# Two of the eight sums over partitions of a modulation vector: accumulating transfers in DRAM instead of TensorE transposes

## The chip, the cores and the metric

The kernel runs on one core of one Trainium2 chip. The metric is the device time of one execution in microseconds (us). Three runs of the kernel before took 1219.54, 1219.89 and 1221.70 us; their median is 1219.89 us. The profile is that of one more execution. Times inside it are us from the start of its span.

## What is computed

The reference is one layer of a diffusion backbone over 512 latent tokens of 1024 channels, with 256 context tokens beside them. Cut to what matters here:

```
mod = silu(c) @ w_mod + b_mod              # 1024 -> 6 * 1024
sh1, sc1, gt1, sh2, sc2, gt2 = split(mod, 6)
x = x + gt1 * token_mixer(modulate(x, norm1_g, sh1, sc1), ...)
x = x + gt2 * conv_ffn(modulate(x, norm2_g, sh2, sc2))
out = rmsnorm(x, final_g)
```

`gt2` is the last 1024 of the 6144 numbers. It is a gate: each of its numbers scales one channel of the ConvFFN's result. So it is needed only at the very end, while its share of the product with `w_mod` can be formed at any time before.

## The kernel before

All matrix products run on TensorE (PE) in float32r, with each operand split into a high part (a cast on ScalarE, ACT) and a low part (a subtraction on VectorE, DVE), so that each product is three matmuls. Weights stream from DRAM on SyncE's queue (SP) in pieces of 512 KB into three buffers `wraw`; `load` (lines 186 to 210) issues a piece, and `split` (line 181) makes `whi` and `wlo` of it. `run` goes through a list of steps and loads each step's weights one or two pieces ahead. The steps' order is written out by hand with `weave`, which deals the items of a second list evenly among those of a first. A scheduler then places the instructions on each engine's queue by its own estimate, except where a step is marked as ordered by hand.

The last two stages matter here. In the **up stage** (`up_step`, t = 0 to 21; matmuls on lines 237, 238 and 240) each step multiplies the normed tokens with two pieces of `w_up`, 48 matmuls with a free size of 512, and DVE and ACT apply a convolution of three taps, an activation and the product of the two halves (lines 1391 to 1395 and 1976 to 1986). In the **down stage** (`down_step`; matmuls on lines 2215 to 2217) seven products follow, in six pieces of weights each, as `w_down` is multiplied by a scheme with fewer products. Sums of its weights were formed earlier, in the attention stage, by accumulating transfers on GpSimd's queue (line 164). The first down weights go through `whi` and `wlo` too, later ones also through `dnraw` and `dnw`.

The second modulation (the last 4096 of the 6144 numbers) is computed on DVE, not on PE: `m_step(i)`, i = 0 to 31, loads a piece of `w_mod`, multiplies its rows by `silu(c)`, one number per partition, and adds up in an accumulator `acc` (a buffer of the tag `tm`, 128 x 512). Four steps make one column group `cg` of 512 columns (lines 794 and 796). What is left is the sum over the 128 partitions. For that PE transposes the four 128 x 128 blocks into a bank of PSUM (line 800), DVE reduces it to four columns of `mod2` (line 802) and adds the bias (line 803). Groups 6 and 7 (i = 24 to 31) hold `gt2`; their steps are dealt among the up steps 0 to 17.

`row_tiles` (from line 2056) makes rows of the gate: it copies and negates the eight columns into `g2c`, transposes them on PE (line 2060), copies the result out of PSUM (line 2061), stores 4 KB to DRAM (`g2_d`, line 2062, printed as `g_d`) and loads them back, spread over all partitions (line 2068, into the tags `q2` and `ssq`, printed as `rowq` and `rowssq`). It also loads two rows of `final_g` (line 2067), the second into a buffer of the tag `tm`. The gate rows are first used in the middle of the down stage, by GpSimd on line 2091.

Of the kernel before, what the change touches and what calls it, by code (L numbers as in the profile page):

```python
# [9 lines left out]
F32 = mybir.dt.float32  # L10
# [3 lines left out]
ALU = mybir.AluOpType  # L14
# [4 lines left out]
P = 128  # L19
# [8 lines left out]
V_BMOD = 0  # L28
# [11 lines left out]
def raw(ap):  # L40
    return ap.bitcast(F32)
# [3 lines left out]
def tile_hybrid_layer(  # L45
# [32 lines left out]
    V, S, G, T = nc.vector, nc.scalar, nc.gpsimd, nc.tensor  # L78
# [5 lines left out]
    dpool = ctx.enter_context(tc.tile_pool(name="dpool", bufs=1, space=DRAM))  # L84
# [25 lines left out]
    def misb():  # L110
        return bank("mis")
# [3 lines left out]
    def tmp(tag):  # L115
        return tpool.tile([P, 512], F32, tag=tag, name=tag, bufs=TMP[tag])
# [27 lines left out]
    for j, t in enumerate((wdn[0], DSUMS[1], DSUMS[2], DSUMS[5], DSUMS[4], wdn[1], wdn[3])):  # L144
        for u in range(DU):
            n = min(2, DK - 2 * u) * HC
# [11 lines left out]
    QUEUED = mybir.DependencyInfo(mybir.DependencyClass.NoSync, mybir.DependencyReason.SCHED_ONLY)  # L158
# [22 lines left out]

    def split(r, n, hi, lo):
        F["cast"] = S.copy(hi[:, :n], r[:, :n])  # L183
        return V.tensor_tensor(lo[:, :n], r[:, :n], raw(hi[:, :n]), ALU.subtract)  # L184

    ELSEWHERE = {}
    SCALED = {("dn", 40), ("dn", 41)}
# [1 line left out]
    def load(key):  # L189
        r, n = load_raw(key)  # L190
        if key[0] == "m":
            return r
        if key in SCALED:
            for z in range(0, n, 512):
                V.tensor_tensor(r[:, z : z + 512], r[:, z : z + 512], rows_["g"][1], ALU.mult)
        if key in ELSEWHERE:
            hi, lo = ELSEWHERE[key]()
            split(r, n, hi, lo)
            return hi, lo
        if key[0] == "dn" and key[1] % 4 > 1:  # L200
            if "dnw" not in F:
                F["dnw"] = hpool.tile([P, 2, 2, 1024], F32R, tag="hll", name="dnw")
            hi, lo = (F["dnw"][:, key[1] % 2, i, :] for i in range(2))
        else:
            hi = wpool.tile([P, 1024], F32R, tag="whi", name="whi", bufs=2)
            lo = wpool.tile([P, 1024], F32R, tag="wlo", name="wlo", bufs=2)
        split(r, n, hi, lo)
        return hi, lo
# [13 lines left out]
    def weave(a, b):  # L222
        r, n, m = [], len(a), len(b)
        for i in range(n):
            r.append(a[i])
            r += b[i * m // n : (i + 1) * m // n]
        return r
# [18 lines left out]
    vec = cpool.tile([P, NV], F32, name="vec")  # L246
# [13 lines left out]
    mod2 = cpool.tile([P, 32], F32, name="mod2")  # L260
# [165 lines left out]
    with tc.tile_pool(name="spool", bufs=1) as sp:  # L426
# [235 lines left out]
        r = {}  # L662
        cq = tmp("te")[:, :LC]
        for j in range(KT):
# [46 lines left out]
            x = ("hi", "lo") if j >= NU else ("hh", "hl")  # L711
# [31 lines left out]
        for n in range(2):  # L743
            for j in range(KT):
                x = ("hi", "lo") if j >= NU else ("hh", "hl")
# [33 lines left out]
        return [("g", i)], fn  # L779

    macc = {}

    def m_step(i):
        cg, kk = i // 4, i % 4

        def fn(r):
            if kk == 0:
                macc[0] = tmp("tm")
            acc = macc[0]
            for u in range(2):  # L790
                k = 2 * kk + u
                sc = csil[:, k, 0:1]
                if k == 0:
                    V.tensor_scalar_mul(acc, r[:, 0:512], sc)
                else:
                    V.scalar_tensor_tensor(acc, r[:, u * 512 : u * 512 + 512], sc, acc, ALU.mult, ALU.add)  # L796
            if kk == 3:
                ps = misb()
                for c in range(4):
                    T.transpose(ps[:, c * P : (c + 1) * P], acc[:, c * P : (c + 1) * P], ident)  # L800
                z = slice(4 * cg, 4 * cg + 4)
                V.tensor_reduce(mod2[:, z], ps.rearrange("p (c q) -> p c q", c=4), axis=AX.X, op=ALU.add)
                V.tensor_tensor(mod2[:, z], mod2[:, z], vec[:, V_BMOD + 16 + 4 * cg : V_BMOD + 20 + 4 * cg], ALU.add)

        return [("m", i)], fn
# [71 lines left out]
    Q, F = {}, {}  # L877
# [1152 lines left out]
    def x1_turn(c):  # L2030

        def fn():
            t = tmp("te")
            V.transpose(t, x1[c // 4][:, c % 4, :])
            for a in range(4):
                o = x1_d[:, c * P + 32 * a : c * P + 32 * a + 32].rearrange("(f i) j -> i f j", i=32)
                nc.sync.dma_start(o, t[32 * a : 32 * a + 32, :].rearrange("i (f j) -> i f j", j=32))

        return [], fn
# [10 lines left out]
    x1_rows = [], x1_load  # L2050
# [3 lines left out]
    rows_ = {}  # L2054

    def row_tiles():
        V.tensor_copy(g2c[:, 0:4], mod2[:, 24:28])
        V.tensor_scalar_mul(g2c[:, 4:8], mod2[:, 28:32], -1.0)
        ps, t = misb(), tmp("te")
        T.transpose(ps[0:8, 0:P], g2c, ident)  # L2060
        V.tensor_copy(t[0:8, 0:P], ps[0:8, 0:P])
        nc.sync.dma_start(g2_d.rearrange("(c p) -> c p", p=P), t[0:8, 0:P])
        tiles = [hpool.tile([P, HC], F32, tag=t, name="row" + t) for t in ("q2", "ssq", "rbc4")] + [tmp("tm")]
        rows_["g"], rows_["f"] = tiles[:2], tiles[2:]
        for i in range(2):
            z = slice(HC * i, HC * i + HC)
            nc.sync.dma_start(rows_["f"][i], fg_d[z].partition_broadcast(P))
            nc.sync.dma_start(rows_["g"][i], g2_d[z].partition_broadcast(P))
# [150 lines left out]
    def down_step(j, u):  # L2219
        tail = j == 6 and u == 2  # L2220

        def fn(*w):
# [40 lines left out]
        + [([("out", o) for o in (5, 6, 7)], out_last), ([], close_c1)]  # L2263
        + weave(
            weave([up_step(t) for t in range(18)], msteps[24:]) + [up_step(t) for t in range(18, NFF)],
            [([], lambda: None)] * 6 + [x1_turn(c) for c in range(8)] + [x1_rows] + [([], lambda: None)] * 4 + [([], row_tiles)] + [([], lambda: None)] * 2,
        )
        + [down_step(j, u) for j in range(7) for u in range(3 if j == 6 else DU)],
        early=("g", 15),
# [86 lines left out]
```

## Time and profile before

| | us |
|---|---|
| median of three runs | 1219.89 |
| the profiled execution | 1219.4 |
| its span, first to last instruction | 1217.6 |
| PE busy | 1208.7 |
| DVE busy | 924.4 |
| ACT busy | 679.6 |
| GpSimd (POOL) busy | 204.8 |

A row of the profile in order of time gives the start, the duration, the engine, the line of the kernel, the operation with its tiles (out <- in), how many such instructions are merged, and in brackets how long the engine was idle before and what released it. PE is the matmul itself and PEld the weight load that runs ahead of it. A matmul's row is longer than the distance to the next row, as matmuls are pipelined. `x2` behind a row means two instructions; its duration is then that of both. SPq is the queue from which SyncE issues transfers. Buffer numbers are left out of names (`x_d` is `x1_d`, `mod` is `mod2`).

### The profile page before, as it was taken

The page shows a single profiled execution, that of the slowest core. Times are in us where ns is not written, and L with a number is a line of the kernel's source. Part 1 is how long each engine was busy: PE and PEld are TensorE (multiplying, and loading weights), DVE is VectorE, ACT ScalarE, POOL GpSimd, SP SyncE. Part 2 cuts the span into 40 slices and gives each one's busy share as a digit, 9 for nine tenths or more (in the row PEclk, how much of TensorE's full clock was granted, in tenths as well). Part 3 has the DMA queues.
Part 4 walks back from the last instruction along what each step waited for, and adds up shares of the span by engine and source line. Part 5 has one row for each costly group of instructions (what it writes and reads, how often), then busy time and mean ns, then how long its engine had stood idle before and what let it go on. Part 6 is the DMA issues. An engine that isn't in the chain of part 4 may idle for free.

```text
span 1217.6 us, 17462 instructions
## 1 busy us (share of the span) xinstructions
PE 1208.7 (99%) x6296; PEld 993.7 (82%) x6296; DVE 924.4 (76%) x1499; ACT 679.6 (56%) x1263; POOL 204.8 (17%) x223
## 2 busy tenths in 40 slices
PE   9999999999999999999999999999999999999997
PEld 6798888888878868778777778888988888888886
DVE  5857888888566688797896867677787777768777
ACT  5557787778544367486575664223534334346653
POOL 0000121100003544252451631000200000000021
PEclk9999999999999999999999999999999999999999
DMA  9645889844758535346376558777265534337652
GB/s 371 259 137 184 160 242 261 170 148 129 175 160 247 169 87 181 108 133 194 104 167 202 172 188 277 233 238 242 55 159 135 190 109 135 119 115 234 193 187 88
DMA packets 122920, 214.71 MB, mean 176 GB/s; under 512 B 26312, under 2 KB 68368, under 8 KB 122832
## 3 DMA queue, kind: packets, MB, share of 16 engines
q1 hardware_dynamic: 110256, 187.09, 49.0%
q0 software_dynamic: 12288, 26.22, 9.5%
q8 instruction: 50, 0.82, 0.3%
q14 instruction: 38, 0.31, 0.1%
q10 hardware_dynamic: 288, 0.27, 0.1%
HBM read 187.26 MB, written 43.85 MB: 190 GB/s over the span
## 4 chain that ended last, share of the span: by engine, by line
PE 96%; DVE 1%; issue 1%; ACT 1%; DMA 1%; POOL 0%; SPq 0%; POOLq 0%; DVEq 0%; ACTq 0%
PE acc L237 20%; PE acc L240 20%; PE acc L238 20%; PE score L958 3%; PE po L1007 3%; PE pt L994 2%; PE mis L580 2%; PE mis L1687 2%; PE mis L1559 2%; PE mis L1695 1%; PE mis L2217 1%; PE mis L2216 1%; PE mis L2215 1%; PE acc L2217 1%; PE acc L2216 1%; PE acc L2215 1%
## 5 line engine op out<-in xcount | busy, mean ns | idle before, releaser
L183 ACT CAST whi<-wraw 128x1024 fp32r<-128x1024 f32 (+1 forms) x115 | 120.3, 1047 | 160.0 <-PE acc L238 107.0
L184 DVE TENSOR_TENSOR wlo<-wraw,whi 128x1024 fp32r<-128x1024 f32 (+1 forms) x115 | 143.6, 1249 | 68.1 <-ACT whi L183 65.6
L237 PE MATMUL acc<-hlh,whi 128*128 128x512 f32 x472 | 194.0, 411 | 0.0
L238 PE MATMUL acc<-hll,whi 128*128 128x512 f32 x472 | 185.0, 392 | 0.0
L240 PE MATMUL acc<-hlh,wlo 128*128 128x512 f32 x472 | 184.9, 392 | 0.0
L237 PE MATMUL acc<-mh,whi 128*128 128x512 f32 x368 | 143.6, 390 | 0.0
L238 PE MATMUL acc<-ml,whi 128*128 128x512 f32 x368 | 143.2, 389 | 0.0
L240 PE MATMUL acc<-mh,wlo 128*128 128x512 f32 x368 | 143.2, 389 | 0.0
L240 PEld LDWEIGHTS acc<-hlh,wlo 128*128 128x128 f32 x472 | 88.6, 188 | 19.6
L237 PEld LDWEIGHTS acc<-hlh,whi 128*128 128x128 f32 x472 | 88.8, 188 | 18.0 <-issue 2.8
L238 PEld LDWEIGHTS acc<-hll,whi 128*128 128x128 f32 x472 | 88.9, 188 | 17.3 <-issue 2.4
L240 PEld LDWEIGHTS acc<-mh,wlo 128*128 128x128 f32 x368 | 69.1, 188 | 14.5
L237 PEld LDWEIGHTS acc<-mh,whi 128*128 128x128 f32 x368 | 69.1, 188 | 14.4
L238 PEld LDWEIGHTS acc<-ml,whi 128*128 128x128 f32 x368 | 69.1, 188 | 14.2
L967 DVE CUSTOM_DVE_ANT_0 p<-score,winm,nsink 128x512 f32<-128x512 f32 (+1 forms) x64 | 51.8, 810 | 15.4 <-PE score L958 13.9
L1392 DVE SCALAR_TENSOR_TENSOR ta<-acc,half,ta 128x511 f32<-128x511 f32 (+1 forms) x66 | 43.8, 664 | 22.6 <-ACT ta L1391 22.4
L1391 ACT ACTIVATE ta<-acc,half 128x512 f32<-128x512 f32 (+1 forms) x66 | 46.7, 708 | 25.2 <-PE acc L240 23.9
L974 ACT ACTIVATE p<-p,mneg 128x512 f32<-128x512 f32 (+1 forms) x64 | 49.7, 777 | 15.4 <-DVE mneg L967 14.8
L164 POOL DMA_DIRECT2D dsum<-wdn x24 | 25.4, 1143 | 193.0 <-DVE wlo L1091 171.7
L1002 DVE TENSOR_TENSOR ptl<-pt,pth 128x512 fp32r<-128x512 f32 x72 | 47.5, 685 | 8.5 <-ACT pth L998 7.7
L796 DVE SCALAR_TENSOR_TENSOR tm<-wraw,csil,tm 128x512 f32<-128x512 f32 x56 | 43.6, 778 | 13.0 <-DMA wraw<-wm 12.3
L237 PE MATMUL acc<-hch,whi 128*128 128x256 f32 x176 | 53.2, 302 | 0.0
(444 smaller groups left out, 2994.0 us busy)
## 6 DMA issues: line engine op xcount, KB each, us to landing
wraw<-wup SPq DMA_DIRECT2D x44, 512.0 KB, 3.6
dsum<-wdn POOLq DMA_DIRECT2D x24, 704.0 KB, 8.9
wraw<-wm SPq DMA_DIRECT2D x32, 512.0 KB, 4.0
fb<-cs_d SPq DMA_DIRECT2D x32, 512.0 KB, 6.6
wraw<-wx SPq DMA_DIRECT2D x24, 512.0 KB, 3.7
wm<-wm SPq DMA_DIRECT2D x16, 512.0 KB, 8.2
wraw<-wz SPq DMA_DIRECT2D x16, 512.0 KB, 4.2
wraw<-wos SPq DMA_DIRECT2D x16, 512.0 KB, 4.7
```

The costliest lines, as they stand in the source:

```text
L183: F["cast"] = S.copy(hi[:, :n], r[:, :n])
L184: return V.tensor_tensor(lo[:, :n], r[:, :n], raw(hi[:, :n]), ALU.subtract)
L237: T.matmul(ps, wh, xh[:, k0 + k, :], start=a, stop=False)
L238: T.matmul(ps, wh, xl[:, k0 + k, :], start=False, stop=False)
L240: T.matmul(ps, wl, xh[:, k0 + k, :], start=False, stop=b)
L796: V.scalar_tensor_tensor(acc, r[:, u * 512 : u * 512 + 512], sc, acc, ALU.mult, ALU.add)
L958: T.matmul(ps[:, o : o + len(z) * P], Q[h][:, b * P : (b + 1) * P], k[:, j, z[0] * P : (z[-1] + 1) * P], start=v == 0 and o % 512 in (0, P ...
L967: V.tensor_tensor_reduce(p[:, :w], d["ps"][i][:, o0 : o0 + w], m, op0=ALU.add, op1=ALU.min, scale=1.0, scalar=nsink[:, h : h + 1], accum_o ...
L974: S.activation(p, p, AF.Exp, bias=d["mneg"][:, i : i + 1], scale=-1.0, accum_out=d["den"][:, i : i + 1])
L1002: V.tensor_tensor(d["ptl"][x], d["pt"][x], raw(d["pth"][x]), ALU.subtract)
L1391: S.activation(o[:, :n], ps[:, :n], AF.Identity, scale=hcol(base_w, stride + i), bias=hcol(base_b, i))
L1392: x = V.scalar_tensor_tensor(o[:, 1:n], ps[:, 0 : n - 1], hcol(base_w, i), o[:, 1:n], ALU.mult, ALU.add)
```

## The change

For the column groups 6 and 7 the sum over partitions is no longer formed on PE and DVE. The accumulator is stored to a tile in DRAM, 128 rows of 512. Then seven transfers on GpSimd's queue each add the upper half of the rows that are left to the lower half, in place: 64 rows, 32, 16, 8, 4, 2 and 1. A ninth transfer loads the one row that remains into four columns of `mod2`. The bias is added by a new function `folded`, on DVE and behind a split: for group 6 in the last m step, for group 7 at the head of `row_tiles`. `row_tiles` itself stands two places later in the list that is dealt among the up steps (21 empty or other items ahead of it instead of 19, of 22).

```diff
 
     def split(r, n, hi, lo):
         F["cast"] = S.copy(hi[:, :n], r[:, :n])
-        return V.tensor_tensor(lo[:, :n], r[:, :n], raw(hi[:, :n]), ALU.subtract)
+        F["sub"] = V.tensor_tensor(lo[:, :n], r[:, :n], raw(hi[:, :n]), ALU.subtract)
+        return F["sub"]
...
     macc = {}
+    FOLDS = {cg: dpool.tile([P, 512], F32, name="fold%d" % cg) for cg in (6, 7)}
+
+    def fold(cg, acc):
+
+        d, n = FOLDS[cg], P // 2
+        G.dma_start(d, acc)
+        while n:
+            G.dma_start(d[0:n, :], d[n : 2 * n, :], accum_op=ALU.add, max_dma_last_dim=512)
+            n //= 2
+        G.dma_start(mod2[:, 4 * cg : 4 * cg + 4], d[0, :].rearrange("(c p) -> p c", p=P))
+
+    def folded(cg):
+        z = slice(4 * cg, 4 * cg + 4)
+        x = V.tensor_tensor(mod2[:, z], mod2[:, z], vec[:, V_BMOD + 16 + 4 * cg : V_BMOD + 20 + 4 * cg], ALU.add)
+        tc.add_manual_dep(x.ins, F["sub"].ins.name, QUEUED, reason="behind a split")
...
-            if kk == 3:
+            if i == 31:
+                folded(6)
+            if kk == 3 and cg in FOLDS:
+                fold(cg, acc)
+            elif kk == 3:
                 ps = misb()
...
     def row_tiles():
+        folded(7)
         V.tensor_copy(g2c[:, 0:4], mod2[:, 24:28])
...
-            [([], lambda: None)] * 6 + [x1_turn(c) for c in range(8)] + [x1_rows] + [([], lambda: None)] * 4 + [([], row_tiles)] + [([], lambda: None)] * 2,
+            [([], lambda: None)] * 6 + [x1_turn(c) for c in range(8)] + [x1_rows] + [([], lambda: None)] * 6 + [([], row_tiles)],
```

**GpSimd, the second chain.** Here are the nine transfers of group 7 on its queue and the instruction behind them (`fold_765` is the tile in DRAM, `mod_94` is `mod2`; shapes are those of the transfers as they are cut). Each of them waits for the one ahead.

```order
L788 DMA fold_765<-tm 128x512
L790 DMA fold_765<-fold_765 256x128
L790 DMA fold_765<-fold_765 128x128
L790 DMA fold_765<-fold_765 64x128
L790 DMA fold_765<-fold_765 32x128
L790 DMA fold_765<-fold_765 16x128
L790 DMA fold_765<-fold_765 16x64
L790 DMA fold_765<-fold_765 16x32
L792 DMA mod_94<-fold_765 128x4x1
L2112 TENSOR_TENSOR te<-te,rowq_10795 128x512
```

Before, the queue had none of these rows: behind the eight subtractions `ml<-ta,mh` of the normalization came the last row, line 2091 there. Nine more rows, for group 6, now stand ahead of the ones shown. On PE the row `mis<-ident,tm 128x128 x4` is gone at the two places where groups 6 and 7 ended; nothing has taken its place.

**DVE and PE at the end of the up stage.** On DVE the last up step before, from the low part of the first down weight:

```order
L184 TENSOR_TENSOR wlo<-wraw,whi 128x1024
L1954 TENSOR_TENSOR fs_8819<-fx_8815,fs_8819 128x256
L1392 SCALAR_TENSOR_TENSOR ta<-acc,half,ta 128x511
L1395 SCALAR_TENSOR_TENSOR ta<-acc,half,ta 128x511
L1977 SCALAR_TENSOR_TENSOR ta<-tb,ta 128x512
```

and the same place now, to the low part of the second down weight:

```order
L184 TENSOR_TENSOR wlo<-wraw,whi 128x1024
L1974 TENSOR_TENSOR fs_8821<-fx_8817,fs_8821 128x256
L1412 SCALAR_TENSOR_TENSOR ta<-acc,half,ta 128x511
L796 TENSOR_TENSOR mod_94<-mod_94,vec 128x4
L1415 SCALAR_TENSOR_TENSOR ta<-acc,half,ta 128x511
L2079 TENSOR_SCALAR g2c<-mod_94 128x4
L1997 SCALAR_TENSOR_TENSOR ta<-tb,ta 128x512
L2082 COPY te<-mis 8x128
L184 TENSOR_TENSOR wlo<-wraw,whi 128x1024
```

The bias add of group 7 (line 796 of the changed kernel), which waits for the ninth transfer, the scaling of `g2c` and the copy of the transposed `g2c` have moved here from the steps of t = 17 and t = 19. On PE the transpose of `g2c` now stands between the last matmul of the up stage and the first of the down stage, where before the two stood side by side:

```order
L241 MATMUL acc<-mh,wlo 128x512
L2081 MATMUL mis<-ident,g2c 8x128
L2236 MATMUL mis<-whi,fs_8820 128x512
L2237 MATMUL mis<-whi,fs_8820 128x512
L2238 MATMUL mis<-wlo,fs_8820 128x512
```

**SP's queue** from the last piece of `w_mod` on, before:

```order
L177 DMA wraw<-wm 128x1024
L177 DMA wraw<-wup 128x1024 x4
L2067 DMA tm<-fg_d 128x512
L177 DMA wraw<-wup 128x1024 x4
L2062 DMA g_d<-te 8x128
L177 DMA wraw<-wdn 128x1024
L2068 DMA rowq_10631<-g_d 128x512
L2068 DMA rowssq<-g_d 128x512
L177 DMA wraw<-wdn 128x1024 x3
L177 DMA dnraw<-wdn 128x512
```

and now:

```order
L177 DMA wraw<-wm 128x1024
L177 DMA wraw<-wup 128x1024 x2
L2088 DMA tm<-fg_d 128x512
L177 DMA wraw<-wup 128x1024 x6
L177 DMA wraw<-wdn 128x1024 x4
L177 DMA dnraw<-wdn 128x512
L2083 DMA g_d<-te 8x128
L177 DMA dnraw<-dsum_75 128x1024
L177 DMA wraw<-wdn 128x1024
L2089 DMA rowq_10795<-g_d 128x512
L2089 DMA rowssq<-g_d 128x512
L177 DMA wraw<-dsum_75 128x1024 x2
```

The row of `final_g` into `tm` has moved ahead of two weight loads, and now waits for the store of `tm` on GpSimd's queue. The store of `g2_d` and the two gate rows stand behind the first four down weights, the gate rows behind the fifth as well.

## The prediction

> **What bounds the kernel now.** I read the page first (busy shares), then the busy time in stretches of the program, then the list of waits, and at last the instructions in order of time around the two places that the change touches.
>
> ```profile
> span 1217.6 us, 17462 instructions
> PE 1208.7 (99%) x6296; PEld 993.7 (82%) x6296; DVE 924.4 (76%) x1499; ACT 679.6 (56%) x1263; POOL 204.8 (17%) x223
> 950.00:1000.00 50.00, 50.00 (x224) 41.36 (x224) 37.86 (x56) 19.94 (x27) 0.00 (x0) 1.00 0.39 128
> 1050.00:1080.00 30.00, 30.00 (x135) 24.81 (x135) 22.11 (x34) 13.06 (x18) 0.00 (x0) 1.00 0.33 107
> 1110.00:1150.00 40.00, 40.00 (x179) 33.10 (x178) 29.96 (x33) 25.77 (x33) 0.00 (x0) 1.00 0.74 238
> ```
>
> The last three rows are stretches: length, then the busy time of PE, PEld, DVE, ACT and POOL, the granted clock (1.00), the DMA share and GB/s. Up stage (950 to 1105) and down stage (1105 to 1209) look alike: PE is busy in all of 50, 30 and 40 us. So a matmul-side instruction taken out there shortens the run by what it costs PE; DVE, ACT, POOL and the transfers matter only where they come so late that PE waits. DVE has 20 to 25% to spare.
>
> **The change, part by part.**
>
> *Eight transposes less on PE.* Two of the eight groups at L800 go, the ones for column groups 6 and 7. Their neighbourhood in order of time:
>
> ```profile
> 954.81 0.39 PE L240 MATMUL acc<-mh,wlo 128*128 128x512 f32 x1
> ...
> 962.29 0.39 PE L240 MATMUL acc<-mh,wlo 128*128 128x512 f32 x1
> 962.53 0.60 PE L800 MATMUL mis<-ident,tm 128*128 128x128 f32 x4
> 962.88 0.48 PE L237 MATMUL acc<-mh,whi 128*128 128x512 f32 x1
> ...
> 966.19 0.39 PE L240 MATMUL acc<-mh,wlo 128*128 128x512 f32 x1
> ```
>
> ```profile
> 1060.71 0.39 PE L240 MATMUL acc<-mh,wlo 128*128 128x512 f32 x1
> 1060.94 0.60 PE L800 MATMUL mis<-ident,tm 128*128 128x128 f32 x4
> ...
> 1064.61 0.39 PE L240 MATMUL acc<-mh,wlo 128*128 128x512 f32 x1
> ```
>
> From the L240 at 954.81 to that at 962.29 are 11 triples, 33 matmuls: 7.48 / 33 = 0.2267 us each. From 962.29 to 966.19 there are 15 matmuls, 15 x 0.2267 = 3.40, but 3.90 us pass: the group costs **0.50 us**, not the 0.60 that its row shows, because matmuls overlap, and some of it lies in a slower pace just behind. From 1060.71 to 1064.61 it is again 15 matmuls in 3.90 us: 0.50. Sum: **-1.0 us**, all on the path. The small transpose of g2c only changes its place; it costs what it cost.
>
> *DVE.* Two reductions of PSUM go, and the two adds of the bias stay. That is work off the path; I count nothing.
>
> *The chain on GpSimd's queue.* Per column group nine transfers, each waiting for the one ahead: the store of acc, seven sums, and the load of four columns into mod2. GpSimd has nothing else to do then:
>
> ```profile
> POOL te L2091 <- DVE te L2113: 290.2, 1, 290.2
> ```
>
> Its next instruction waits 290.2 us for the down stage, so nothing is held up behind the nine. The question is only whether the load into mod2 lands before DVE reaches the bias add, since a late one stops DVE, and with it PE. The second chain (column group 7) has the shorter time. It starts when the last accumulation ends:
>
> ```profile
> 1044.92 1.54 DVE L796 SCALAR_TENSOR_TENSOR tm<-wraw,csil,tm 128x512 f32<-128x512 f32 x2 [0.16 <-DMA wraw<-wm]
> 1063.97 0.15 DVE L803 TENSOR_TENSOR mod<-mod,vec 128x4 f32<-128x4 f32 x1
> 1064.76 0.16 DVE L2058 TENSOR_SCALAR g2c<-mod 128x4 f32<-128x4 f32 x1
> 1102.18 0.74 DVE L1392 SCALAR_TENSOR_TENSOR ta<-acc,half,ta 128x511 f32<-128x511 f32 x1
> 1102.96 0.75 DVE L1395 SCALAR_TENSOR_TENSOR ta<-acc,half,ta 128x511 f32<-128x511 f32 x1
> 1105.08 0.39 PE L2215 MATMUL mis<-whi,fs 128*128 128x512 f32 x1
> ```
>
> Start 1044.92 + 1.54 = 1046.46. In the new order the bias add stands between L1392 and L1395 of the last up step, so at 1102.18 + 0.74 = 1102.92: 56.5 us, less 0.5 since the group at 1060.94 is gone. Behind it come L1395 (0.75) and the scaling of g2c (0.16); 1102.92 + 0.15 + 0.75 + 0.16 = 1103.98, while PE wants its transpose at 1105.08, so 1.1 us more is free: the chain may take about **57 us** at no cost. What it takes, the trace shows only by relatives:
>
> ```profile
> dsum<-wdn POOLq DMA_DIRECT2D x24, 704.0 KB, 8.9
> fb<-cs_d SPq DMA_DIRECT2D x32, 512.0 KB, 6.6
> L1444 POOL DMA_DIRECT2D xs_d<-xb x32: 582/620/692, 376.3 to 412.5; - x32
> DMA to landing us min/median/max: 1.8/3.5/7.8
> 392.84 4.93 POOL L1444 DMA_DIRECT2D xs_d<-xb  x8 [4.81 <-DVE xb L1435]
> 399.08 0.77 POOL L1453 DMA_DIRECT2D xs<-xs_d  x1 [1.31 <-DMA xs_d<-xb]
> ```
>
> Rows 1 to 4 give the time from issue to landing. Small stores on this queue (rows 3 and 4) take 1.8 to 7.8, in the middle 3.5. Rows 5 and 6 show one step of a dependent pair: the last store is issued at 392.84 + 4.93 - 0.62 = 397.15, a reader at 399.08, a step of 1.9 if it waited for the last one. Sums of 704 KB are among the transfers of row 1 (8.9); here they are 128 KB and less. I take 3.5 for the store and for each sum, being nearest in size, and 6.6 (row 2, also many short pieces) for the load of columns: 3.5 + 24.5 + 6.6 = 34.6 us, over at 1081, with 22 us to spare. Ends: 9 x 1.8 = 16 us, no cost; and 7.8 + 7 x 8.9 + 7.8 = 77.9 us, 21 us of stall. Chain 6 starts 98 us earlier, before 949, and its add stands near 1059, so even 77.9 us fit.
>
> A row first: the 620 ns of an issue (row 3 above) were measured while DVE worked beside it. The Trainium skill, SBUF — State Buffer, speaks against the change in the sections "A bandwidth-pool intuition that's wrong (but worth ruling out)" and "Who interferes with whom": a transfer issued by GpSimd whose descriptors are kept back by a DVE copy took about 3100 ns where it takes 620 alone. By that the nine would take an estimated 22 us more, 57 in all, just at the limit: no loss yet, but nothing to spare. The same section names copy, cast and tensor_scalar as the operations that do so and leaves tensor_tensor out, and the trace sides with this: 582 to 692 ns, no row near 3100.
>
> *SP's queue.* The row load of final_g now stands two weight loads earlier and waits for the store out of tm instead of for PE; the store of g2 and the two gate rows move from the up stage into the start of the down stage.
>
> ```profile
> 1046.49 11.65 SPq L177 DMA_DIRECT2D wraw<-wup  x4
> 1061.57 0.33 SPq L2067 DMA_DIRECT2D tm<-fg_d  x1
> 1083.81 0.34 SPq L2062 DMA_DIRECT2D g_d<-te  x1
> 1086.03 0.33 SPq L2068 DMA_DIRECT2D rowq<-g_d  x1
> rowq<-g_d SPq DMA_DIRECT2D x1, 256.0 KB, 4.0
> rowssq<-g_d SPq DMA_DIRECT2D x1, 256.0 KB, 4.2
> ```
>
> The store out of tm should land by 1046.46 + 3.5 = 1050 (1054.3 at 7.8). Two of the four loads in the first row now come behind it, and the last of the four leaves at 1057.8 today; even 1054.3 lets it leave then, and today SP stands until 1061.57 without a gap on PE: I count nothing. SP waited 1086.03 - 1083.81 = 2.2 us from the store of g2 to its first reader. Now that store leaves at about 1105.8, once DVE has copied the transposed g2c, so the rows leave at about 1108, 0.5 MB right behind the load of the fifth down weight:
>
> ```profile
> 1107.39 0.33 SPq L177 DMA_DIRECT2D wraw<-wdn  x1
> 1111.37 1.05 ACT L183 CAST whi<-wraw 128x1024 fp32r<-128x1024 f32 x1 [1.17 <-DMA wraw<-wdn]
> 1113.34 1.22 DVE L184 TENSOR_TENSOR wlo<-wraw,whi 128x1024 fp32r<-128x1024 f32 x1
> 1115.96 0.39 PE L2215 MATMUL mis<-whi,fs 128*128 128x512 f32 x1
> ```
>
> That weight is the tightest: ACT waits for its landing, DVE is done at 1114.56, and PE needs the low part in its third matmul, at 1115.96 + 2 x 0.2267 = 1116.41. If the rows push the landing back by 512 KB at the 238 GB/s of the stretch, 2.2 us, the cast ends at 1114.6 and the low part at 1115.9: still in time, I take 0. Were it the whole 4.2 us of a row's landing, the low part would be ready at 1111.37 + 4.2 + 1.05 + 1.22 = 1117.84, 1.4 us late; a gain is excluded, as nothing leaves the bus there.
>
> **Sum.** The profiled execution took 1219.4 (span 1217.6 and 1.8 around it). 1219.4 - 1.0 = 1218.4; the median of the runs, 1219.89, lies 0.5 above that execution, so **1218.9**.
>
> **The rivals.**
> - *The chain is late.* Place: the bias add of group 7 on DVE, with g2c's transpose on PE at the head of the down stage behind it. With 3.5 and 6.6 for the first and last transfer it decides from (57 - 10.1) / 7 = 6.7 us per sum. At 8.9 the chain takes 72.4, 15.4 too long: 1218.9 + 15.4 = **1234.3**. For it: a sum must read two operands, and the only sums in the trace are among the slow row. Against it: those move 704 KB, and a small store is seen to land in 1.8.
> - *Gate rows in the crowd.* 1.4 us of stall at the fifth down weight: **1220.3**. For it: a DMA share of 0.74, and ACT already waits there for a landing. Against it: 1.85 us of slack, and the rows leave behind that weight, not ahead of it.
> - *The gain doesn't arrive.* If transfers, not free buffers, set the pace at the start of the down stage, PE arrives 1.0 us early and waits: **1219.9**. Against it: PE is busy in all of 40 us, and SP's loads there are released by DVE.
>
> **How the numbers follow.** The forecast gets 0.70, the late chain 0.13, the crowded rows 0.10, the lost gain 0.07. About 0.2%, 2.4 us, is what a measurement of this kernel can tell from no change (1217.5 to 1222.3). Within it lie the rows, the lost gain, 0.01 of the late chain (late by under 3 us) and 0.66 of the forecast, whose other 0.04 is the chance that scatter or a dearer transpose carries it past the bound: same 0.84, faster 0.04, slower 0.12. The range 1217.8 to 1221.0 takes in the forecast with the scatter of the runs and both small rivals; the late chain up to 21 us stays outside, within the 2 in 10.
>
> **What would show it.** PE rows: six groups of four transposes instead of eight, and PE still without idle time from 950 to 1209. GpSimd's queue: a step of about 3.5 us, the load into mod2 done near 1081; a wait of DVE's bias add on a DMA of more than a few tenths, and PE idle ahead of g2c's transpose, would prove the late chain. The gate rows: leaving near 1107, and the fifth cast landing by 1113.5; a PE gap near 1115 would prove the crowd. I'd be wrong altogether if the sums cost a time that doesn't shrink with their size.

## The result, and the profile after

The changed kernel takes **1218.28 us** (median of 21 runs, 1217.51 to 1219.53); the kernel before took 1219.81 in 21 runs beside it (1219.06 to 1221.70). The ratio is 0.9987, with a 95% interval of 0.9981 to 0.9993: 1.5 us less, between 0.9 and 2.3. The forecast was 1218.9, within 0.2% of before. The profiled execution took 1217.93 (before 1219.4).

The page's head of the changed kernel, then two of its stretches (columns as in the prediction):

```profile
span 1216.2 us, 17466 instructions
PE 1207.5 (99%) x6288; PEld 992.7 (82%) x6288; DVE 922.6 (76%) x1497; ACT 679.5 (56%) x1263; POOL 219.1 (18%) x241
```

```profile
1050.00:1080.00 30.00, 30.00 (x134) 24.85 (x133) 22.17 (x34) 12.46 (x18) 6.47 (x8) 1.00 0.44 121
1110.00:1150.00 40.00, 40.00 (x179) 33.10 (x178) 29.66 (x33) 26.55 (x33) 0.00 (x0) 1.00 0.76 253
```

PE has eight instructions fewer and is still busy in all of 30 and 40 us; GpSimd has eighteen more and works 6.47 us in the first stretch, where it did nothing before. Where the groups of transposes stood, the matmuls now follow each other without a break (instructions of PE in order of time; L241 is the line that was L240):

```profile
954.67 0.39 PE L241 MATMUL acc<-mh,wlo 128*128 128x512 f32 x1
...
965.55 0.39 PE L241 MATMUL acc<-mh,wlo 128*128 128x512 f32 x1
...
1063.47 0.39 PE L241 MATMUL acc<-mh,wlo 128*128 128x512 f32 x1
...
1208.66 0.28 PE L2238 MATMUL mis<-wlo,fs 128*128 128x256 f32 x1
```

These are the matmuls that the kernel before starts at 954.81, 966.19, 1064.61 and (its last) 1209.79. From the first to the second it took 11.38 us and now 10.88: **0.50** for group 6. From the second to the third 98.42, now 97.92: **0.50** for group 7. From the third to the last 145.18, now 145.19: nothing. The first of them starts 0.14 earlier already; the lead is 0.15 at 752, ahead of all that the change touches, so it isn't part of the change. The last 0.27 of the 1.4 us by which the span is shorter come behind the last matmul and the last issue of an output (both 1.13 earlier); nothing here shows that they are part of it. So 1.0 us is shown to be the change, and the rest of the 1.5 is within what the runs' interval leaves open.

The chain on GpSimd's queue (in brackets the idle time ahead of an instruction, and what ended it):

```profile
1046.15 0.56 POOL L788 DMA_DIRECT2D fold<-tm  x1 [68.54 <-DVE tm L812]
1050.87 0.96 POOL L790 DMA_DIRECT2D fold<-fold  x1 [4.16 <-DMA fold<-tm]
1056.42 0.82 POOL L790 DMA_DIRECT2D fold<-fold  x1 [4.58 <-DMA fold<-fold]
...
1072.39 0.76 POOL L790 DMA_DIRECT2D fold<-fold  x1 [2.34 <-DMA fold<-fold]
1074.72 0.82 POOL L792 DMA_DIRECT2D mod<-fold  x1 [1.57 <-DMA fold<-fold]
```

The store takes 4.7 (6.5 in the first chain), the seven sums (1074.72 - 1050.87) / 7 = 3.41 each, between 2.3 and 5.6, and the load lands 3.5 after its issue (3.3 and 3.8 in the two chains): over at 1078.2, 32 us after the start. DVE comes to the bias add long after that and finds it ready (no bracket on its first row), and PE does not wait for the small transpose:

```profile
1101.58 0.15 DVE L796 TENSOR_TENSOR mod<-mod,vec 128x4 f32<-128x4 f32 x1
1104.13 0.28 DVE L2082 COPY te<-mis 8x128 f32<-8x128 f32 x1 [0.23 <-PE mis L2081]
```

And the start of the down stage, with the gate rows now in it (the first of the two; the second leaves at 1107.26):

```profile
1106.89 0.32 SPq L2089 DMA_DIRECT2D rowq<-g_d  x1
1110.75 1.06 ACT L183 CAST whi<-wraw 128x1024 fp32r<-128x1024 f32 x1 [1.69 <-DMA wraw<-wdn]
1112.08 1.21 DVE L184 TENSOR_TENSOR wlo<-wraw,whi 128x1024 fp32r<-128x1024 f32 x1
1115.28 0.39 PE L2238 MATMUL mis<-wlo,fs 128*128 128x512 f32 x1
```

ACT waits 1.69 for the fifth weight's landing (1.17 before), DVE is done at 1113.29, and PE takes the low part at 1115.28: 2.0 us to spare.

### The profile page after: what moved, and what is told of

Read it like the earlier page. It is cut to its first block, busy times and chain, and to the rows that moved or that the text cites. A ratio compares the mean times of both kernels' runs of the same rounds, so it can differ in the third digit from the quotient of the medians.

```text
span 1216.2 us, 17466 instructions
## 1 busy us (share of the span) xinstructions
PE 1207.5 (99%) x6288; PEld 992.7 (82%) x6288; DVE 922.6 (76%) x1497; ACT 679.5 (56%) x1263; POOL 219.1 (18%) x241
## 4 chain that ended last, share of the span: by engine, by line
PE 96%; DVE 1%; issue 1%; ACT 1%; DMA 1%; POOL 0%; SPq 0%; POOLq 0%; DVEq 0%; ACTq 0%
PE acc L238 20%; PE acc L241 20%; PE acc L239 20%; PE score L978 3%; PE po L1027 3%; PE pt L1014 2%; PE mis L581 2%; PE mis L1707 2%; PE mis L1579 2%; PE mis L1715 1%; PE mis L2237 1%; PE mis L2236 1%; PE mis L2238 1%; PE acc L2237 1%; PE acc L2236 1%; PE acc L2238 1%
## 5 line engine op out<-in xcount | busy, mean ns | idle before, releaser
L184 DVE TENSOR_TENSOR wlo<-wraw,whi 128x1024 fp32r<-128x1024 f32 (+1 forms) x115 | 143.6, 1249 | 70.6 <-ACT whi L183 68.4
L241 PE MATMUL acc<-hlh,wlo 128*128 128x512 f32 x472 | 184.9, 392 | 0.0
L241 PE MATMUL acc<-mh,wlo 128*128 128x512 f32 x368 | 143.2, 389 | 0.0
L241 PEld LDWEIGHTS acc<-hlh,wlo 128*128 128x128 f32 x472 | 88.6, 188 | 19.5
L241 PEld LDWEIGHTS acc<-mh,wlo 128*128 128x128 f32 x368 | 69.1, 188 | 14.4
L1022 DVE TENSOR_TENSOR ptl<-pt,pth 128x512 fp32r<-128x512 f32 x72 | 47.5, 685 | 8.4 <-ACT pth L1018 7.9
L812 DVE SCALAR_TENSOR_TENSOR tm<-wraw,csil,tm 128x512 f32<-128x512 f32 x56 | 43.6, 778 | 11.6 <-DMA wraw<-wm 10.9
```

The source lines that it names most:

```text
L184: F["sub"] = V.tensor_tensor(lo[:, :n], r[:, :n], raw(hi[:, :n]), ALU.subtract)
L241: T.matmul(ps, wl, xh[:, k0 + k, :], start=False, stop=b)
L1022: V.tensor_tensor(d["ptl"][x], d["pt"][x], raw(d["pth"][x]), ALU.subtract)
```

## The experiments

My theory: only the PE time of the removed transposes counts, 0.50 us per group; the eighteen transfers, the later rows and DVE's part cost and bring nothing as long as the chain is over in its 57 us. Runs scatter by more than half a microsecond, so I also use a sharper measure, as above: the time between two starts of the same pair of matmuls, the one of 954.81 and the last. What comes ahead of the change's place and what scatters at the end drops out of it.

| kernel | first, last start | between | against before | median of runs, ratio (95% interval) |
|---|---|---|---|---|
| before | 954.81, 1209.79 | 254.98 | | |
| changed | 954.67, 1208.66 | 253.99 | -0.99 | 1218.28, 0.9987 (0.9981 to 0.9993) |
| no transfers | 955.44, 1209.42 | 253.98 | -1.00 | 1218.55, 0.9991 (0.9982 to 1.0000) |
| rows later, nothing else | 955.32, 1210.30 | 254.98 | 0.00 | 1219.70, 0.9998 (0.9989 to 1.0006) |
| transposes twice | 954.48, 1210.25 | 255.77 | +0.79 | 1220.59, 1.0008 (0.9999 to 1.0017) |
| sixteen more sums | 955.42, 1209.40 | 253.98 | -1.00 | 1218.51, 0.9991 (0.9982 to 1.0000) |
| sixteen copies in the chain | 955.07, 1231.62 | 276.55 | +21.57 | 1241.74, 1.0184 (1.0170 to 1.0199) |
| six copies in the chain | 955.39, 1209.37 | 253.98 | -1.00 | 1218.35, 0.9990 (0.9981 to 0.9999) |
| rows at the old place | 954.84, 1208.82 | 253.98 | -1.00 | 1219.14, 0.9995 (0.9986 to 1.0004) |

### Taking away one part, or doing one alone

**No transfers.** In place of the chain:

```
+    V.tensor_copy(mod2[:, 4 * cg : 4 * cg + 4], acc[:, 0:4])
```

> The changed kernel without any of the eighteen transfers: each of the two groups' four columns are copied out of the accumulator by DVE, so the sum over partitions (of groups 6 and 7 only) is left out. Theory (only the PE time of the eight transposes counts, 0.50 us per group; the transfers, the later rows and DVE cost and bring nothing): the same as the changed kernel, -1.0 us against before, PE starts at the head of the down stage within 0.2 us of the changed kernel's. Rival (the transfers cost something on the bus or DVE's port): faster than the changed kernel by what they cost, -1.5 to -2.5 us against before.

1218.55, and 253.98 us between the two matmuls, 0.01 from the changed kernel. So the eighteen transfers cost nothing in that stretch, neither on the bus nor at DVE, and the rival is out.

**Rows later, nothing else.** The kernel before with

```
-  ... + [x1_rows] + [([], lambda: None)] * 4 + [([], row_tiles)] + [([], lambda: None)] * 2
+  ... + [x1_rows] + [([], lambda: None)] * 6 + [([], row_tiles)]
```

> The kernel before with only the call of row_tiles moved two places later; the transposes stay. Theory: 0.0 us against before, PE starts in the down stage within 0.2 us of before's. Rival (the move of the rows and of the small transpose is part of the gain): -0.3 to -0.5 us. Rival of the crowd: the rows behind the fifth down weight cost up to +1.4 us.

254.98, the same as before to 0.01. The small transpose of g2c can be seen to move: PE's rows between 1083 and 1105 start 0.13 earlier against the rest, and the 0.13 is given back at 1105. So the transpose costs 0.13 at either place, and the gate rows in the down stage cost nothing.

**Transposes twice.** The kernel before with

```
-  for c in range(4):
+  for c in [0, 1, 2, 3] * (2 if cg > 5 else 1):
```

> The kernel before with the four transposes of groups 6 and 7 issued twice, the second time into the same bank. Theory: +0.5 us per group, +1.0 us against before, PE's rows behind 962 later by 0.5 and behind 1061 by 1.0. Rival (a group costs PE only the 0.25 us by which its neighbours move, or nothing, and the measured gain came from elsewhere): 0 to +0.5 us.

PE around group 6:

```profile
954.48 0.39 PE L240 MATMUL acc<-mh,wlo 128*128 128x512 f32 x1
...
962.19 1.03 PE L800 MATMUL mis<-ident,tm 128*128 128x128 f32 x8
...
966.25 0.39 PE L240 MATMUL acc<-mh,wlo 128*128 128x512 f32 x1
```

966.25 - 954.48 = 11.77, 0.39 more than the 11.38 of before, and 98.81 to the mark behind group 7 in place of 98.42. +0.79 in all where +1.0 was expected: a transpose more in a row costs 0.10 us, and of the 0.50 of a group 0.10 are for going from matmuls to transposes and back, paid once. The rival "0 to +0.5" is out.

**Rows at the old place.** The changed kernel with row_tiles where it was called before (the reverse of the second diff).

> The changed kernel with row_tiles called where the kernel before calls it, so that the bias add of group 7 stands between two adds of the up step before the last two, at 1079.9, with some 1.1 us more before PE would miss the small transpose; the chain is over at 1078.2 by the changed kernel's trace, at about 1081 in the run with sixteen more sums. Theory: at the limit, 0 to +2 us against the changed kernel. Rival (the move is needed for another reason, such as the gate rows on SP's queue): the same time with the chain in time, or more than +3.

The end of the chain on GpSimd's queue and the bias add on DVE, in this run's trace:

```profile
1075.14 0.82 POOL L792 DMA_DIRECT2D mod<-fold  x1 [1.55 <-DMA fold<-fold]
```

```profile
1079.98 0.15 DVE L796 TENSOR_TENSOR mod<-mod,vec 128x4 f32<-128x4 f32 x1
```

The load left at 1075.14, and at 3.5 us more it landed at 1078.6, 1.3 ahead of the bias add, which did not wait. 253.98 again, as the changed kernel. So in the profiled execution the move of the rows is not needed; it makes the reserve 23 us (1101.58 - 1078.2) instead of 1.3. The runs lie 0.9 above the changed kernel's, but the medians of their spans are 1216.7 and 1216.5, so most of it is not between the first and the last instruction, where a late chain would show. Whether the chain is late in a few of these runs (the longest span is 1218.8, against 1217.8) is left open.

### How long may the chain be?

**Sixteen more sums.** Ahead of the load of group 7:

```
+  for k in range(16 if cg == 7 else 0):
+      G.dma_start(d[k + 1 : k + 2, :], d[k : k + 1, :], accum_op=ALU.add, max_dma_last_dim=512)
```

> The changed kernel with sixteen more dependent sums of one row (2 KB) ahead of the load in the second chain, 2.5 us each as the last sums of the changed kernel's trace, so 32 + 40 = 72 us in place of 32. Theory (the chain is free as long as it is over within about 57 us of 1046.5): DVE's bias add waits until about 1118 and PE ahead of the small transpose, +15 us against the changed kernel (+14 against before); the excess is chain minus 57. Rival (the wait for a late chain is hidden by work that can go ahead of the small transpose): 0 to +3 us.

This was a miss of mine: the load needs none of these sums, and it was put ahead of them. It left behind the first of them (GpSimd's instructions in order of time, in this run):

```profile
1078.27 0.76 POOL L793 DMA_DIRECT2D fold<-fold  x1 [2.18 <-DMA fold<-fold]
1078.77 1.09 POOL L794 DMA_DIRECT2D mod<-fold  x1
```

So the run doesn't test the limit. It shows only that sixteen more transfers on that queue, the last of them issued at 1134.2, cost nothing (253.98). They follow each other at (1134.19 - 1078.27) / 15 = 3.73 us; the 2.87 from which the two expectations below start isn't what this trace shows. That the copies then came near it (2.93 each with sixteen, 2.56 with six) was luck.

**Sixteen, and six copies.** Copies forth and back between two rows, so that the load must wait:

```
+  for k in range(16 if cg == 7 else 0):      # 6 in the other kernel
+      G.dma_start(d[1 - k % 2 : 2 - k % 2, :], d[k % 2 : k % 2 + 1, :])
```

> The changed kernel with sixteen copies of one row (2 KB, forth and back within the group's DRAM tile) between the last sum and the load of the second chain, so that the load itself has to wait for them. At the 2.87 us per step that the sixteen small sums of the run before showed: 16 x 2.87 = 46 us more, the load into mod2 done near 1078.2 + 46 = 1124, where DVE's bias add stands in line at 1101.6 and PE's transpose can wait another 1.1. Theory: +21 us against the changed kernel, +20 against before (+15 to +28). Rival (the wait is hidden by other work of PE): 0 to +3 us against the changed kernel.

> The same with six copies: 6 x 2.87 = 17 us more, load done near 1095.5, 6 us ahead of the bias add. Theory: 0.0 us against the changed kernel, -1.0 against before. Rival (each step of a chain takes PE time somewhere): 6/16 of what the sixteen copies cost.

With sixteen, on GpSimd, DVE and PE:

```profile
1046.49 0.57 POOL L788 DMA_DIRECT2D fold<-tm  x1 [68.50 <-DVE tm L814]
...
1121.80 0.80 POOL L794 DMA_DIRECT2D mod<-fold  x1 [2.27 <-issue]
```

```profile
1124.38 0.17 DVE L798 TENSOR_TENSOR mod<-mod,vec 128x4 f32<-128x4 f32 x1 [12.58 <-DMA mod<-fold]
```

```profile
1103.98 0.39 PE L241 MATMUL acc<-mh,wlo 128*128 128x512 f32 x1
1124.81 0.38 PE L2083 MATMUL mis<-ident,g2c 128*8 128x128 f32 x1 [20.44 <-DVE g2c L2081]
1125.41 0.63 PE L2239 MATMUL mis<-whi,fs 128*128 128x512 f32 x1
...
1128.40 0.63 PE L2240 MATMUL mis<-wlo,fs 128*128 128x512 f32 x1
```

The chain takes 1124.38 - 1046.49 = 77.9 us, by chance just the prediction's upper end, for which it gave 21 us of stall: PE waits 20.4. The whole loss is 276.55 - 253.98 = 22.6, because PE behind the wait goes at (1128.40 - 1125.41) / 7 = 0.427 us per matmul in place of 0.2267 for some four microseconds. The granted clock falls from 1.00 to 0.50 between 1108 and 1109, four microseconds behind PE's last matmul, and is 1.00 again from 1129, four microseconds behind the first one after the wait. The Trainium skill, TensorE: Matmul & The Clock Gate, "What's actually happening", says that the array falls to half its clock after an idle window of about 3.4 us and comes back after as long a busy one; this trace fits both, with about four each.

One thing besides the copies differs here: the scheduler put the bias add behind the first splits of the down stage, so DVE went on working until 1111.8 and then waited 12.58. It was the transpose standing in PE's queue that stopped PE, not a stopped DVE.

With six copies nothing is lost (253.98; 1218.35): the load lands near 1091.12 + 3.4 = 1094.5, 47.5 us after the start of the chain. So 47.5 us are free, and 77.9 lose 20.4 of waiting, which puts the limit near 57.5, where the prediction had it, and the late chain stopped PE as told.

### Can more groups go the same way?

If a group is worth 0.50 us, groups 2 and 3 offer another 1.0: GpSimd is idle from 742 to 854, and their columns are needed at 846 and later. Measure here: between the matmul that the changed kernel starts at 752.01 and its last, 456.65 us (before 457.63). This stretch repeats less well: the kernel with sixteen more sums, the same up to group 7, has 457.15. Half a microsecond decides nothing in this table.

| kernel | between | against the changed kernel | median of runs, ratio to before (95% interval) |
|---|---|---|---|
| groups 2, 3, 6, 7 | 468.58 | +11.93 | 1230.52, 1.0092 (1.0078 to 1.0106) |
| groups 3, 6, 7 | 459.57 | +2.92 | 1222.51, 1.0020 (1.0011 to 1.0029) |
| four groups, two chains alternating | 463.85 | +7.20 | 1226.29, 1.0047 (1.0034 to 1.0061) |
| four groups, accumulators of their own | 477.74 | +21.09 | 1239.30, 1.0161 (1.0147 to 1.0175) |

**Four groups.**

```
-  FOLDS = {cg: ... for cg in (6, 7)}
+  FOLDS = {cg: ... for cg in (2, 3, 6, 7)}
   def vectors():
+      folded(2)
+      folded(3)
```

> The changed kernel with groups 2 and 3 summed by transfers as well (their chains start near 770 and, behind the first on the queue, near 802; 32 us each, over near 834; the bias adds stand ahead of the scaling vector at 846). GpSimd is idle from 742 to 854 there. Theory: another 0.50 us per group, -1.0 us against the changed kernel, -2.0 against before. Rival (at a DMA share of 0.76, against 0.39 and 0.33 at groups 6 and 7, the chains are slower or delay weights): chains over after 846 and DVE waits, or SP's loads land later; +1 us or more against the changed kernel.

GpSimd, and then DVE and PE at the end of group 3, in order of time:

```profile
807.63 0.84 POOL L792 DMA_DIRECT2D mod<-fold  x1 [2.61 <-DMA fold<-fold]
808.46 0.58 POOL L788 DMA_DIRECT2D fold<-tm  x1
```

```profile
811.14 0.48 DVE L810 TENSOR_SCALAR tm<-wraw,csil 128x512 f32<-128x512 f32 x1 [8.69 <-DMA fold<-tm]
...
813.72 1.22 DVE L184 TENSOR_TENSOR wlo<-wraw,whi 128x1024 fp32r<-128x1024 f32 x1
```

```profile
814.99 0.79 PE L241 MATMUL acc<-yh,wlo 128*128 128x512 f32 x1 [4.89 <-DVE wlo L184]
```

There is one accumulator, tm. Group 3's store stood behind the whole chain of group 2 in GpSimd's queue and left at 808.46, so DVE waited 8.69 us to begin group 4, and behind it stood the low part of a weight, for which PE waited 4.89. The chains were over by about 840, in time: it is not their length that costs. My expectation had priced only that. Of the 11.93, PE loses 7.3 at this place (5.0 waiting and 2.3 behind it, at a granted clock of 0.50), 1.7 ahead of it (DVE waits 2.49 for group 2's store there) and 3.8 behind it, at 813 to 820 of the changed kernel's time.

**Group 3 alone beside 6 and 7**, with folded(3) in vectors; its store meets an empty queue.

> The changed kernel with group 3 alone added to groups 6 and 7, so that its store meets an empty queue. In the changed kernel's trace the accumulator is done at 798.1 and DVE writes it again at 805.7; a store of 4.4 to 5 us after its issue ends by 804. Theory (what the run with groups 2 and 3 lost came from the one accumulator buffer, held by a store that stood behind the other chain on GpSimd's queue): no wait of DVE for the store beyond a few tenths, -0.5 us against the changed kernel, -1.5 against before. Rival (a chain beside the denser transfers of this stage costs by itself): +2 us or more against the changed kernel, with PE waiting for weights.

The 0.50 of the transposes come, and 3.4 are lost right after. DVE's order at the end of group 3, first in the changed kernel, then here:

```profile
802.13 0.69 DVE L1807 TENSOR_TENSOR tb<-acc,ld 128x512 f32<-128x512 f32 x1
...
804.00 1.22 DVE L184 TENSOR_TENSOR wlo<-wraw,whi 128x1024 fp32r<-128x1024 f32 x1
805.74 0.48 DVE L810 TENSOR_SCALAR tm<-wraw,csil 128x512 f32<-128x512 f32 x1
```

```profile
805.35 0.49 DVE L810 TENSOR_SCALAR tm<-wraw,csil 128x512 f32<-128x512 f32 x1 [1.40 <-DMA fold<-tm]
...
806.54 0.69 DVE L1807 TENSOR_TENSOR tb<-acc,ld 128x512 f32<-128x512 f32 x1
...
807.87 1.22 DVE L184 TENSOR_TENSOR wlo<-wraw,whi 128x1024 fp32r<-128x1024 f32 x1
```

Two things differ: DVE waits 1.40 us for the store, and the first step of group 4 (L810) now stands ahead of the operands that PE needs (L1807, L184), where it stood behind them. With the transposes and their reduction gone from this place, the scheduler orders DVE's work so. The store took 6.8 us (798.77 to 805.56), not the 4.4 to 5 that I had given it. But this place costs PE only 0.7. The other 2.7 go later, where DVE waits 1.95 and 1.19 us for pieces of `w_mod` (L812); the work on the second of them now stands ahead of PE's operand (L1807), where it stood behind (DVE, then PE):

```profile
817.33 0.75 DVE L812 SCALAR_TENSOR_TENSOR tm<-wraw,csil,tm 128x512 f32<-128x512 f32 x1 [1.19 <-DMA wraw<-wm]
817.99 0.69 DVE L1807 TENSOR_TENSOR tb<-acc,ld 128x512 f32<-128x512 f32 x1
```

```profile
821.12 0.50 PE L238 MATMUL acc<-mh,whi 128*128 128x512 f32 x1 [1.90 <-ACT mh L1809]
```

So the theory of the store alone is out. The rival's number came (+2.92), but PE's long wait stands behind DVE's new order; whether the chain's transfers delay those pieces as well isn't shown.

**The two chains alternating**: group 2's last three sums and its load are held on GpSimd's queue behind group 3's store.

```
+  tc.add_manual_dep(x.ins, last[-1].ins.name, QUEUED, reason="behind the other chain")
```

> The kernel with four groups by transfers, but the last three sums and the load of group 2 are put behind group 3's store on GpSimd's queue and alternate with group 3's sums; the number of transfers and the bytes are the same. Theory (the buffer held by the queued store cost the 10 us): the 8.7 us wait of DVE for that store falls to under 1, the wait of 2.5 behind group 2's store stays with PE gaps of about 1 us: between -1.0 and +1.5 us against the changed kernel. Rival (36 transfers on a busy bus cost it): still +8 to +12 us.

The 8.69 us wait is gone; at its place DVE waits 3.98 for a piece of `w_mod`. PE loses 1.6 there in place of 7.3, but 2.9 in place of 1.7 ahead of it and still 3.6 behind it, so the loss falls from 11.93 to 7.20. Neither the theory's range nor the rival's 8 to 12 holds: the store's place in the queue explains a part only.

**Accumulators of their own** for groups 2 and 3, so that nobody waits for their stores:

```
+  own = {2: "rbc4", 3: "ssq"}.get(cg)
+  macc[0] = hpool.tile([P, 512], F32, tag=own, name="macc") if own else tmp("tm")
```

> The kernel with four groups by transfers, but the accumulators of groups 2 and 3 lie in two other buffers that are free until the down stage's rows, so that DVE never waits for their stores; transfers, bytes and queue order are those of the run with four groups. Theory (the lost time of the runs with groups 2 and 3 is DVE waiting for the one accumulator buffer, 2.5 and 8.7 us, and the weight loads that this makes late): no wait of DVE on those stores, four groups gain 0.50 each, -2.0 us against before, -1.0 against the changed kernel. Rival (eighteen more transfers at a DMA share of 0.76 delay weights and accumulations by themselves): PE still waits for weights between 785 and 830, +1 to +6 us against before.

A mistake of mine governs this run: the buffer for group 2 was not free. ACT's r_s lies in it, and with it the whole stage waits for group 2's store:

```profile
770.76 0.58 ACT L320 COPY r_s<-mis 128x512 f32<-128x512 f32 x1 [11.20 <-DMA fold<-macc]
```

PE loses 14.7 us there in one wait, and about 2 more behind it at a granted clock of 0.50. Group 3's accumulator was free, and no wait of DVE for that store is seen; yet PE still loses 5.3 us of matmul time between the marks that the changed kernel has at 812 and 825 (18.45 in place of 13.16), with DVE waiting for the second modulation's own weights (some 1.5 of the 5.3 are again a granted clock of 0.50):

```profile
DVE tm L813 <- DMA wraw<-wm: 6.4, 3, 3.0
DVE macc L813 <- DMA wraw<-wm: 6.0, 4, 3.6
```

(DVE's list of waits from 760 to 850: us, times, longest. The changed kernel has 2.1 us in 2 such waits there.) The same stretch costs PE 2.7, 3.8 and 3.6 us in the three kernels above. So holding the buffer isn't all of it. Whether the rest is DVE's new order or the denser transfers was not separated. The pieces of `w_mod` do not land later (median 4.4 us from issue to landing from 797 to 857, against 4.5 in the changed kernel from 780 to 840), which speaks for the order. No version here beats the changed kernel.

**Group 1**, in the stage of the state updates, where GpSimd works; folded(1) stands ahead of g1h.

> The changed kernel with group 1 summed by transfers as well, in the stage of the state updates, where GpSimd is busy in 40 to 65% of the time with work that others wait for. Its nine transfers stand between GpSimd's operations, each waiting some 2.5 to 5 us for the one ahead, and hold up what stands behind. Theory (a chain is free only on a queue with nothing behind it): -0.5 for the transposes, but 8 waits of about 3 us of which a third to all reach PE, +5 to +25 us against the changed kernel. Rival (GpSimd's work there has slack): -0.5 us.

1226.40, ratio 1.0056 (1.0042 to 1.0070), 8.0 us above the changed kernel between the matmul at 655.06 and the last (561.59 against 553.60). The lists of PE's and DVE's waits from 640 to 720 in this run (us, times, longest) begin with:

```profile
PE mis L1707 <- DVE st L1582: 5.1, 1, 5.1
```

```profile
DVE st L1582 <- POOL st L1581: 6.0, 2, 3.1
```

One of the places on GpSimd's queue:

```profile
672.28 0.80 POOL L790 DMA_DIRECT2D fold<-fold  x1 [2.77 <-DMA fold<-fold]
672.84 1.33 POOL L1581 TENSOR_TENSOR st<-st,eT 128x512 f32<-128x512 f32 x1
```

GpSimd's state updates (L1581) stood behind sums that waited for sums, DVE waited for them, and PE for DVE. Behind PE's wait of 5.1 the granted clock is 0.51 from 677 to 684. The rival, that GpSimd has slack there, is out.

## Why the prediction was right, step by step

- **"Eight transposes less on PE", -1.0 us, all on the path.** Right to 0.01 us: 0.50 and 0.50, in the changed kernel and in every kernel without the two groups. The doubled transposes add a finer split: four more cost 0.40, so 0.10 of a group is left for the change of work on PE.
- **"The small transpose of g2c ... costs what it cost."** Right: 0.13 at both places. **DVE off the path:** right; the reductions gone from DVE bring nothing beyond the 1.0.
- **"The chain on GpSimd's queue", 34.6 us, 22 to spare.** Measured 32.1. The terms were off against each other: the store 4.7 for 3.5, the sums 3.41 for 3.5, the load 3.5 for 6.6. The load was priced by a row of 512 KB and moves 2 KB. That the total came so near is in part luck. The allowance of 57 us held: a chain of 47.5 us cost nothing, and one of 77.9 cost 20.4 of waiting for the 21 that were worked out. What the price of a late chain lacked is the slow clock behind the wait, about 2 us.
- **"I'd be wrong altogether if the sums cost a time that doesn't shrink with their size."** This sign came in part. In the second chain the steps are 5.55, 3.77, 2.56, 3.95, 2.59, 3.10 and 2.33 us from 64 rows down to one: they shrink over the first two halvings; below that no shrinking shows above the scatter. It did no harm, because the sum had priced all seven alike, at 3.5, and had 22 us to spare; the sign was too strict for the prediction that it was to test.
- **Transfers held back by DVE.** No issue of a sum took longer than 0.97 us (the line of the sums in the changed kernel's trace; ns min/median/max):

```profile
L790 POOL DMA_DIRECT2D fold<-fold x14: 754/776/974, 954.7 to 1072.4; - x14
```

  So the rule that the prediction weighed, from the Trainium skill, SBUF — State Buffer, "A bandwidth-pool intuition that's wrong (but worth ruling out)", did not decide here: no issue is near its 3100 ns, as the prediction expected for DVE's operations of this stage.

- **"SP's queue", 0.** Right, and shown twice: the rows moved alone (0.00) and the changed kernel with the rows at the old place (0.01) differ in nothing but reserve. The rows left at 1106.9 where 1108 was given, and landed 5.9 and 6.7 us later, not 4.0 and 4.2, so the crowd is there; the slack at the fifth weight was enough.
- **The rival "the gain doesn't arrive"** falls with the last mark: 1.14 earlier at 1063.47, and 1.13 at the last matmul.
- **From 1218.9 to 1218.28.** The runs show 0.5 us more of a gain than the 1.0. No step accounts for it. In the five kernels that lack the transposes and have no stall, the medians lie 0.65 to 1.5 below before, and the medians of the spans 1.2 to 1.5 (1216.5 to 1216.8 against 1218.0), while the matmuls say 1.0 in each. A part may lie behind the last matmul: from its start to the end of the span are 7.4 to 7.6 us in the profiles of these five, and 7.6 to 7.9 in the three with the transposes. With one profile each this stays open.

## What to carry to other kernels

Work taken off the engine that is never idle is worth its pace in the instruction stream (here 0.50 for a row that says 0.60), and a chain of nine transfers was free here where it had an idle queue, slack at its end, and a source buffer that nobody wanted back soon. Look for what stands behind each of the three before the next group is moved: the same edit one stage earlier lost 2.9 to 11.9 us. The queue and the buffer made a part of that; the order of the waiting engine is the likely rest. To measure half a microsecond, compare the times between two starts of the same matmuls in the profiles; here that repeated to 0.01 us from 955 on, where runs scatter by 0.6. Check on unchanged kernels that it does: from 752 on it scattered by up to 0.5.

## What the runs showed of the hardware

- A wait of PE can cost more than its length, and one wait's length doesn't tell whether it will. Behind 20.4 us, and behind the 4.89 us in the run with four groups, matmuls went at 0.427 us each for about four microseconds; behind the 1.90 us wait in the run with group 3 they went at 0.23 almost at once. But in the run with four groups they went at 0.43, with a granted clock of 0.50 from 830 to 833, behind two waits of 1.02 and 0.59 only:

```profile
828.24 0.49 PE L238 MATMUL acc<-mh,whi 128*128 128x512 f32 x1 [1.02 <-ACT mh L1809]
829.33 0.50 PE L239 MATMUL acc<-ml,whi 128*128 128x512 f32 x1 [0.59 <-DVE ml L1810]
...
830.30 0.63 PE L239 MATMUL acc<-ml,whi 128*128 128x512 f32 x1
...
832.44 0.63 PE L238 MATMUL acc<-mh,whi 128*128 128x512 f32 x1
```

  The same two matmuls wait 1.27 and 0.58 in the run with accumulators of their own, with the same slow pace behind them, and 1.0 and 0.6 in the run with alternating chains, without it. What decides between them was not found.
- Small sums in DRAM don't get cheap with size: from 128 KB down to 2 KB they land 2.0 to 5.3 us after issue, 2.5 in the middle; the sixteen sums of 2 KB in the run with them 2.0 to 6.3, 3.1 in the middle; and the sixteen copies of 2 KB 1.7 to 4.9.
- In the run with group 1, GpSimd worked without a pause from 684.2 to 692.6, and DVE's product of two SBUF operands that began at 685.92 took 4.74 us, where the same line takes 0.69 in the middle (the line's row in that run; ns min/median/max, then first and last start):

```profile
L1567 DVE TENSOR_TENSOR xw<-xs,TD x24: 682/686/4735, 421.8 to 685.9; 128x512 f32<-128x512 f32 x24
```

The Trainium skill, SBUF — State Buffer, "Who interferes with whom", says that such a DVE operation contends with GpSimd's reads and that the second to start is blocked. This row agrees; it is one instance, and it was not tried by itself.
